# Decay exponents as sixteen products of 128 rows, with the weighing on VectorE

## The chip, the cores and the metric

The kernel runs on one core of a Trainium2 chip. The metric is the device time of one execution in microseconds. The names of the engines are those of the profile: PE is TensorE (its weight loads are PEld), DVE is VectorE, ACT is ScalarE, POOL is GpSimd, SP is SyncE, which issues most of the DMA transfers.

## The reference

One encoder layer over 256 positions and 2048 channels, in float32: a mixer, a gated convolutional MLP and an embedding block, each between RMS norms. Only the mixer matters here. One projection of the normalised input gives z (1024 channels), xbc (1536), dt (32) and u (1024). u goes through pooling windows and a small product per group. xbc goes through a convolution over five positions and a silu and is divided into xs (1024 channels, 16 heads of 64), B and C (two groups of 128 states each). Then comes a scan in chunks of 128 positions, once in each direction:

```python
da = dt * a                                   # a < 0
acum = jnp.cumsum(da, axis=-1)                # within a chunk of 128
cb = jnp.einsum("bclgn,bcsgn->bcgls", cmc, bmc)
seg = acum[..., :, None] - acum[..., None, :]
decay = jnp.exp(jnp.where(causal, seg, -jnp.inf))
y_diag = jnp.einsum("bcgls,bcgels,bcsgep->bclgep", cb, decay, xdt)   # xdt = xs * dt
decay_to_end = jnp.exp(acum[..., -1:] - acum)
states = jnp.einsum("bclgn,bcgel,bclgep->bcgepn", bmc, decay_to_end, xdt)
...
y = y_fwd + y_bwd + xs * d_skip               # then times silu(z), normed, projected
```

So every chunk, head and direction needs a 128x128 matrix of exponentials of differences of running sums.

## The kernel before, in words

**Arithmetic.** A float32 product is made of three faster products. `split` turns each weight block of 128x1024 into a high half, a cast on ACT (L150), and a low half, a subtraction on DVE (L151). PE then multiplies high by high, high by low and low by high. All of these go through the helper `mm`, so L87 is the line of nearly every product and they are told apart by the names of their outputs.

**Order.** The program's stages follow one another: the products for dt and u (`dtu`); three slabs of xbc, each of 512 channels and 192 products of 128x256, in the order 2 (B and C), 0, 1 (xs); z, in eight pairs of 24 products of 128x512; then the gate and norm of y, the output projection, the MLP and the embedding block. Each engine runs its own queue in an order that a scheduler fixed when the program was built. Small work is put among a stage's products by hand: `aside` takes one entry of the list `work` after each quarter of a slab, and after each pair of z, and runs its jobs.

**Buffers.** PSUM is divided into six tiles for the stages' sums (`main`) and two for everything else (`misc`): `seg`, `pool_mix`, `pool_map`, `cb`, `xs_turn`, `yo` and `yd` all use these two in turn. In SBUF there are 13 pages of 128x2048, five buffers each for high and low halves, and three raw ones.

**The mixer's small work.** After `dtu`, dt and `da` are made by small operations on DVE. `decays` makes the four vectors of decays to the chunk's ends (`dps`, `dec`). The exponents are made in eight parts of four heads each. `seg_prep(i)`, on POOL, multiplies masks with the high and low part of `da` (four operations of 128x512, L562), and `seg(i)` adds up both directions in one PSUM tile with four products; ACT takes the exponential into E (L571). For a pair of positions one of the two directions' exponents is zero there, since the masks select the other.

A slab's end is `xbc`: two products with the norm (`xr`, L409, DVE), a convolution of 16 instructions on DVE (L426), a tanh on ACT and one more DVE operation (L628). `cb` (L600) makes the products of C and B, masked by direction into `cbm`. `weigh(t, g)` makes `w`, the two directions' masked products times their dt: the first step on POOL (L634, 128x1024), then eight DVE operations of 128x128 (L639), then E times w (L643). `xs_turn` turns xs to have positions on partitions. `far(t)` weighs xs with the decay to the chunk's end (`xd`, POOL, L650), `skip(t)` starts y with xs times d (POOL, L654). `mix(t, g)` adds the part from the other chunk (`yo`, one product) and from the own (`yd`, eight products) to y.

The lists of jobs say where this stands. In slab 2: `seg_prep` 0 to 3, `pool_mix`, `decays`, `seg` 0. In slab 0: `seg_prep` 4 to 7, `seg` 1 to 4, `pool_map`, `cb`, `weigh(0, 0)`. In slab 1: `seg` 5 to 7, `xs_turn` of slab 0, the other three `weigh`. In z: after the fourth pair `xs_turn` of slab 1, after the fifth `far` and `skip`, then `mix`.

Of the kernel before, what the change touches and what calls it, by code (L numbers as in the profile page):

```python
# [11 lines left out]
F32 = mybir.dt.float32  # L12
F32R = mybir.dt.float32r
AF = mybir.ActivationFunctionType
ALU = mybir.AluOpType

P = 128
# [4 lines left out]
H = 16  # L22
# [29 lines left out]
def build(nc, a, out):  # L52
# [5 lines left out]
    with tile.TileContext(nc) as tc, \  # L58
# [12 lines left out]
        def page(name, dtype=F32):  # L71
            return gp.tile([P, 2048], dtype, tag="pg", bufs=13, name=name)
# [10 lines left out]
        def misc(name):  # L83
            return pc.tile([P, 512], F32, tag="misc", name=name)

        def mm(o, lhsT, rhs, start, stop):
            nc.tensor.matmul(o, lhsT, rhs, start=start, stop=stop, skip_group_check=True)  # L87


        ep = early.enter_context(tc.tile_pool(name="early", bufs=1))  # L90
# [18 lines left out]

        xt = [ep.tile([P, V_SCW + L], F32, name="xt0")] + [page(f"xt{i}") for i in (1, 2)]  # L110
        vt = cp.tile([P, V_N - V_SCW], F32, name="vt")
        small = ep.tile([P, 80 + 512], F32, name="small")

        last, sums_ = {}, {}

# [12 lines left out]

        last["dma"] = load(xt[0], a["x_cols"][:, :V_SCW + L])
        dtb, alog, dsk = small[:, :32], small[:, 32:64], small[:, 64:80]  # L130
        mask = small[:, 80:].rearrange("p (m f) -> p m f", m=4)

        def vec(i):
            return xt[0][:, i:i + 1] if i < V_SCW else vt[:, i - V_SCW:i - V_SCW + 1]
# [306 lines left out]
        for u in range(0, NK, 2):  # L441
            r = [wp.tile([P, 2048], F32, tag="raw", bufs=3, name=f"dtur{u}") if u else r0, page(f"dtur{u + 1}")]
# [37 lines left out]
        with tc.issue_after(half[0]), tc.issue_after(half[1]):  # L480
            xs_ = [page(f"x{t}") for t in range(2)]
            for t in range(2):
                load(xs_[t], x[t * P:(t + 1) * P, :])
            rx = row_rstd("rx", xs_)
            m_gt, m_lt = (ep.tile([P, P], F32R, name=n) for n in ("m_gt", "m_lt"))
            nc.vector.tensor_copy(m_gt, mask[:, 2, :])
            nc.vector.tensor_copy(m_lt, mask[:, 3, :])
            aneg = ep.tile([P, 32], F32, name="aneg")
            nc.scalar.activation(aneg, alog, AF.Exp)
            nc.gpsimd.tensor_scalar(aneg, aneg, -1.0, None, op0=ALU.mult)  # L490


            pt = page("pt")[:, :512].rearrange("p (k t) -> p k t", k=2)
            load(pt, a["p_t"])
            pth = cp.tile([P, 2, L], F32R, name="pth")
            ptl = cp.tile([P, 2, L], F32R, name="ptl")
            nc.scalar.copy(pth, pt)
            nc.vector.tensor_sub(ptl, pt, pth.bitcast(F32))
# [32 lines left out]
        nc.vector.tensor_scalar(e3, e3, 2.0, None, op0=ALU.mult)  # L531
        nc.vector.scalar_tensor_tensor(dtf, dtf, 0.0, e3, op0=ALU.max, op1=ALU.add)
        da = ep.tile([P, 2, 32], F32, name="da")
        dah = ep.tile([P, 2, 32], F32R, name="dah")
        dal = ep.tile([P, 2, 32], F32, name="dal")
        nc.vector.tensor_tensor(da, dt, aneg.unsqueeze(1).to_broadcast([P, 2, 32]), op=ALU.mult)
        nc.vector.tensor_copy(dah, da)
        nc.vector.tensor_sub(dal, da, dah.bitcast(F32))

# [8 lines left out]
                nc.gpsimd.tensor_mul(dec[:, d, :], dec[:, d, :], dt[:, d, d * H:(d + 1) * H])  # L550


        ee = [page(f"E{t}") for t in range(2)]
        steps = {}

        def seg_prep(i):
            t, q = divmod(i, 4)
            ap_ = page(f"ap{i}", F32R).rearrange("p (a h l) -> p a h l", a=4, h=4)
            for j in range(4):
                d, src = j // 2, (dah.bitcast(F32), dal)[j % 2]  # L560
                hs = slice(d * H + 4 * q, d * H + 4 * q + 4)
                nc.gpsimd.tensor_tensor(ap_[:, j], src[:, t, hs].unsqueeze(2).to_broadcast([P, 4, P]),  # L562
                                        mask[:, d, :].unsqueeze(1).to_broadcast([P, 4, P]), op=ALU.mult)
            steps[i] = ap_

        def seg(i):
            t, q = divmod(i, 4)
            sps, ap_ = misc(f"seg{i}"), steps.pop(i)
            for j in range(4):
                mm(sps, (m_gt, m_lt)[j // 2], ap_[:, j].rearrange("p h l -> p (h l)"), j == 0, j == 3)  # L570
            nc.scalar.activation(ee[t][:, q * 512:(q + 1) * 512], sps, AF.Exp)  # L571


        cat = Panel.__new__(Panel)
# [23 lines left out]
        xs = page("xs")  # L598
# [32 lines left out]
        def weigh(t, g):  # L631

            w = mid(f"w{t}{g}")
            nc.gpsimd.tensor_tensor(w.rearrange("p (h l) -> p h l", h=8),  # L634
                                    cbm[:, 1, g, t, :].unsqueeze(1).to_broadcast([P, 8, P]),
                                    dt[:, t, H + 8 * g:H + 8 * g + 8].unsqueeze(2).to_broadcast([P, 8, P]),
                                    op=ALU.mult)
            for h in range(8):
                nc.vector.scalar_tensor_tensor(w[:, h * P:(h + 1) * P], cbm[:, 0, g, t, :],  # L639
                                               dt[:, t, 8 * g + h:8 * g + h + 1], w[:, h * P:(h + 1) * P],  # L640
                                               op0=ALU.mult, op1=ALU.add)
            es = ee[t][:, g * 1024:(g + 1) * 1024]
            nc.vector.tensor_mul(es, es, w)  # L643

        def by_head(ap_, n=H):
            return ap_.rearrange("p (h c) -> p h c", h=n)

        def far(t):
            xd[t] = page(f"xd{t}")[:, :1024]
            nc.gpsimd.tensor_tensor(by_head(xd[t]), by_head(xs[:, t * 1024:(t + 1) * 1024]),  # L650
                                    dec[:, t, :].unsqueeze(2).to_broadcast([P, H, 64]), op=ALU.mult)

        def skip(t):
# [3 lines left out]
        def mix(t, g):  # L657
            c0 = t * 1024 + g * 512
            s = 1 - t
            po = misc(f"yo{t}{g}")  # L660
            mm(po, cbm[:, 2, g, s, :], xd[s][:, g * 512:(g + 1) * 512], True, True)
            tm = mid(f"ym{t}{g}")[:, :512]
            nc.vector.tensor_tensor(by_head(tm, 8), by_head(po, 8),
                                    dec[:, 2 + s, 8 * g:8 * g + 8].unsqueeze(2).to_broadcast([P, 8, 64]), op=ALU.mult)
            nc.gpsimd.tensor_add(y[:, c0:c0 + 512], y[:, c0:c0 + 512], tm)
            pd = misc(f"yd{t}{g}")
            for h in range(8):
                mm(pd[:, h * 64:(h + 1) * 64], ee[t][:, (8 * g + h) * P:(8 * g + h + 1) * P],
                   xs[:, c0 + h * 64:c0 + (h + 1) * 64], True, True)
            nc.vector.tensor_add(y[:, c0:c0 + 512], y[:, c0:c0 + 512], pd)  # L670

        def job(f, *args):
            return lambda: f(*args)

        xd = {}
        work.extend([
            [job(seg_prep, 0)],
            [job(seg_prep, 1), job(pool_mix, 0), job(pool_mix, 1)],
            [job(seg_prep, 2), job(pool_mix, 2), job(pool_mix, 3), job(decays)],
            [job(seg_prep, 3), job(seg, 0)],  # L680
        ])
        bc = xbc(2)
        work.extend([
            [job(seg_prep, 4), job(seg, 1), job(pool_map, 0), job(pool_map, 1)],
            [job(seg_prep, 5), job(seg, 2), job(cb, bc, 0), job(cb, bc, 1)],
            [job(seg_prep, 6), job(seg, 3), job(pool_map, 2), job(pool_map, 3)],
            [job(seg_prep, 7), job(seg, 4), job(weigh, 0, 0)],
        ])
        xa = xbc(0)
        work.extend([  # L690
            [job(seg, 5), job(weigh, 0, 1)],
            [job(seg, 6), job(xs_turn, xa, 0)],
            [job(seg, 7), job(weigh, 1, 0)],
            [job(weigh, 1, 1)],
        ])
        xb = xbc(1)
        y = page("y")
# [1 line left out]

        work.extend([  # L700
            [],
            [],
            [],
            [job(xs_turn, xb, 1)],
            [job(far, 1), job(skip, 0), job(far, 0), job(skip, 1)],
            [job(mix, 0, 0)],
# [291 lines left out]
def laid_out(a):  # L998

    def cols(*vs):  # L1000
        return np.concatenate([v.reshape(-1, P).T for v in vs], axis=1)

    return {
        "x_cols": np.concatenate([cols(a["mix_norm_pre"][0]),
                                  a["x"][0].T.reshape(NK, P, L).transpose(1, 0, 2).reshape(P, NK * L)], axis=1),
        "p_t": a["p"][0, 0].T.reshape(2, P, L).transpose(1, 0, 2),
        "columns": np.concatenate([
            cols(a["ssd_conv_w"][0], a["ssd_conv_b"][0], a["ssd_norm"][0], a["pool_scale"][0], a["ffn_norm_pre"][0],
                 a["ffn_conv_w"][0], a["ple_norm_pre"][0], a["ffn_conv_b"][0]),
            np.broadcast_to(np.concatenate([a[n][0].reshape(-1) for n in ("ssd_dt_bias", "ssd_a_log", "ssd_d")]),  # L1010
                            (P, 80)),
            masks().transpose(1, 0, 2).reshape(P, 4 * P)], axis=1),
    }


def masks():
    j = np.arange(P)[:, None]
    l = np.arange(P)[None, :]
    return np.stack([j <= l, j >= l, j > l, j < l]).astype(np.float32)


def constants():
# [17 lines left out]
```

## Time and profile before

| | |
|---|---|
| median of three runs | 1142.09 us (1141.17 to 1142.82) |
| profiled execution, its own time | 1140.26 us |
| its span | 1138.5 us |
| mean granted clock of TensorE | 0.995 |
| PE busy | 1115.9 us, 98% of the span |
| DVE busy | 935.8 us, 82% |
| ACT busy | 637.6 us, 56% |
| POOL busy | 128.9 us, 11% |

The span is the time from the first to the last recorded instruction of the profiled execution; 1.76 us lie around it, and the median of the runs is 1.83 us above this execution. The busy shares are means over stages with different limits. The stages that the change touches lie between 40 and 200 us: `dtu` ends at about 52 us, the slabs of xbc run to 151.59, and z to about 190. The chain that ended last is the work followed back from the last instruction, at each step to what released it.

### The profile page before, as it was taken

How to read it: one execution, taken by the hardware profiler on the slowest of the kernel's cores; microseconds unless marked ns; L12 is line 12 of the kernel's file. 1: busy time of each engine (PE TensorE's matmuls, PEld its weight loads, DVE VectorE, ACT ScalarE, POOL GpSimd, SP SyncE). 2: the span in 40 equal slices, each digit the busy share in tenths (PEclk: the TensorE clock that was granted, in tenths of full speed). 3: DMA queues.
4: the chain of work that ended last, by engine and by line, in shares of the span. 5: the costliest groups of instructions: out<-in, count | busy, mean ns of one | idle time of the engine just before them, and what ended most of it. 6: DMA issues, size and time to landing. Idle time of an engine off the chain costs nothing.

```text
span 1138.5 us, 15770 instructions
## 1 busy us (share of the span) xinstructions
PE 1115.9 (98%) x5982; PEld 962.5 (85%) x5982; DVE 935.8 (82%) x1277; ACT 637.6 (56%) x869; POOL 128.9 (11%) x124
## 2 busy tenths in 40 slices
PE   9998999999999999999999999999999999998996
PEld 9997987888888888888888888888888888886775
DVE  6579896699888877877877778867799999998795
ACT  7533543555674554544545545545677777776672
POOL 0274504200110100000000000000000000102001
PEclk9999999999999999999999999999999999999999
DMA  9952347545699999998999898966985589985673
GB/s 359 341 184 75 112 151 263 200 164 187 240 311 332 328 325 313 320 294 299 333 335 313 291 323 309 323 218 223 352 286 184 176 301 344 343 277 193 203 236 107
DMA packets 145419, 297.97 MB, mean 262 GB/s; under 512 B 5440, under 2 KB 98496, under 8 KB 137536
## 3 DMA queue, kind: packets, MB, share of 16 engines
q1 hardware_dynamic: 144784, 295.56, 76.4%
q0 software_dynamic: 272, 1.05, 0.5%
q8 instruction: 47, 0.77, 0.3%
q10 hardware_dynamic: 288, 0.36, 0.1%
q14 instruction: 28, 0.23, 0.1%
HBM read 266.54 MB, written 30.41 MB: 261 GB/s over the span
## 4 chain that ended last, share of the span: by engine, by line
PE 91%; DVE 5%; ACT 1%; DMA 1%; POOL 1%; issue 1%; DVEq 0%; POOLq 0%; ACTq 0%
PE va L87 22%; PE ga L87 21%; PE dna L87 15%; PE woa L87 7%; PE gt L87 4%; PE dtu L87 4%; PE z L87 4%; PE xbc L87 3%; PE dns L87 3%; DVE cv L426 2%; PE dn0s L87 1%; PE dn1s L87 1%; PE ple L87 1%; DMA gt04t<-gts 1%; DVE w L639 1%
## 5 line engine op out<-in xcount | busy, mean ns | idle before, releaser
L87 PE MATMUL ga<-wox,ug_0h 128*128 128x512 f32 x352 | 125.6, 395 | 0.0
L87 PE MATMUL ga<-wox,ug_1h 128*128 128x512 f32 x352 | 125.1, 394 | 0.0
L87 PE MATMUL va<-wox,uv_1h 128*128 128x512 f32 x352 | 124.8, 394 | 0.0
L87 PE MATMUL va<-wox,uv_0h 128*128 128x512 f32 x352 | 124.8, 394 | 0.0
L87 PE MATMUL ga<-wox,ug_1l 128*128 128x256 f32 x352 | 99.3, 282 | 0.0
L87 PE MATMUL ga<-wox,ug_0l 128*128 128x256 f32 x352 | 99.3, 282 | 0.0
L87 PE MATMUL va<-wox,uv_1l 128*128 128x256 f32 x352 | 99.2, 282 | 0.0
L87 PE MATMUL va<-wox,uv_0l 128*128 128x256 f32 x352 | 99.2, 282 | 0.0
L87 PEld LDWEIGHTS va<-wox,uv_1h 128*128 128x128 f32 x352 | 66.2, 188 | 14.8
L87 PEld LDWEIGHTS va<-wox,uv_0h 128*128 128x128 f32 x352 | 66.2, 188 | 14.8
L87 PEld LDWEIGHTS ga<-wox,ug_0h 128*128 128x128 f32 x352 | 66.2, 188 | 14.7
L87 PEld LDWEIGHTS ga<-wox,ug_1h 128*128 128x128 f32 x352 | 66.2, 188 | 14.7
L865 POOL TENSOR_TENSOR fc<-fc,rfb 128x1024 f32<-128x1024 f32 x11 | 28.0, 2546 | 438.6 <-ACT fc L864 438.6
L87 PEld LDWEIGHTS ga<-wox,ug_0l 128*128 128x128 f32 x352 | 66.3, 188 | 0.1
L87 PEld LDWEIGHTS ga<-wox,ug_1l 128*128 128x128 f32 x352 | 66.3, 188 | 0.0
L87 PEld LDWEIGHTS va<-wox,uv_0l 128*128 128x128 f32 x352 | 66.3, 188 | 0.0
L87 PEld LDWEIGHTS va<-wox,uv_1l 128*128 128x128 f32 x352 | 66.3, 188 | 0.0
L87 PE MATMUL dna<-dn_0h,hs 128*128 128x512 f32 x176 | 54.8, 394 | 0.0
L87 PE MATMUL dna<-dn_1h,hs 128*128 128x512 f32 x176 | 54.6, 393 | 0.0
L233 DVE TENSOR_TENSOR dnb<-dnb 128x1024 f32<-128x1024 f32 x22 | 28.0, 1271 | 16.1 <-DMA dnb<-w_ffn_down 16.1
L87 PEld LDWEIGHTS dna<-dn_1h,hs 128*128 128x128 f32 x176 | 33.1, 188 | 7.7
L87 PEld LDWEIGHTS dna<-dn_0h,hs 128*128 128x128 f32 x176 | 33.0, 188 | 7.6
(1866 smaller groups left out, 3136.0 us busy)
## 6 DMA issues: line engine op xcount, KB each, us to landing
dnb<-w_ffn_down SPq DMA_DIRECT2D x22, 1024.0 KB, 10.2
dns<-dnb SPq DMA_DIRECT2D x20, 1024.0 KB, 7.3
dn0r<-w_ffn_down SPq DMA_DIRECT2D x11, 1024.0 KB, 5.8
dn1r<-w_ffn_down SPq DMA_DIRECT2D x11, 1024.0 KB, 7.4
zr<-w_in SPq DMA_DIRECT2D x8, 1024.0 KB, 5.1
dtur<-w_in SPq DMA_DIRECT2D x14, 528.0 KB, 8.8
wo0r<-w_out SPq DMA_DIRECT2D x7, 1024.0 KB, 5.5
wo1r<-w_out SPq DMA_DIRECT2D x6, 1024.0 KB, 5.7
```

Source lines behind the costliest of these rows:

```text
L87: nc.tensor.matmul(o, lhsT, rhs, start=start, stop=stop, skip_group_check=True)
L233: nc.vector.tensor_add(v[:, 0:2], v[:, 0:2], v[:, 1::2])
L426: nc.vector.scalar_tensor_tensor(o[:, lo:hi], i[:, lo + d:hi + d], vec(wcol + j * wstep + f), o[:, lo:hi], op0=ALU.mult, op1=ALU.add)
L639: nc.vector.scalar_tensor_tensor(w[:, h * P:(h + 1) * P], cbm[:, 0, g, t, :], dt[:, t, 8 * g + h:8 * g + h + 1], w[:, h * P:(h + 1) * P], ...
L865: nc.gpsimd.tensor_tensor(cv.rearrange("p (f t) -> p f t", f=4), cv.rearrange("p (f t) -> p f t", f=4), rfb.unsqueeze(1).to_broadcast([P, ...
```

## The change

The exponents are written as differences of running sums. `seg_sums` makes these sums once: four products of 64 rows (`cps`) from `da4`, which holds da four times over and, for the second direction, negated. Two pages hold operands of 128 rows: `seg_x` with the sums' high and low parts and with ones, `seg_w` likewise with signs; their upper 64 rows are zero, so that products have the full 128 rows. Each is filled by ACT. Then each `seg(i)` is two products of 128x512, one for each direction, into two `misc` tiles; ACT copies the first to E, DVE takes the minimum of the two, and ACT the exponential. `seg_prep` goes, as do m_gt, m_lt, dah and dal. The first step of `weigh`, and `far`, go from POOL to DVE. `yo` is tied, in the order in which instructions are issued, behind the product that precedes it in the program. The jobs are dealt out anew.

```diff
 def mm(o, lhsT, rhs, start, stop):
-    nc.tensor.matmul(o, lhsT, rhs, start=start, stop=stop, skip_group_check=True)
+    last["pe"] = ins(nc.tensor.matmul(o, lhsT, rhs, start=start, stop=stop, skip_group_check=True))
...
-small = ep.tile([P, 80 + 512], F32, name="small")
+small = ep.tile([P, 89 + 512], F32, name="small")
...
+low, among, four = small[:64, 592:593], small[:64, 593:597], small[:64, 597:601]
...
-m_gt, m_lt = (ep.tile([P, P], F32R, name=n) for n in ("m_gt", "m_lt"))
-nc.vector.tensor_copy(m_gt, mask[:, 2, :])
-nc.vector.tensor_copy(m_lt, mask[:, 3, :])
+seg_w = page("seg_w", F32R)
+nc.scalar.activation(seg_w[64:], xs_[0][64:], AF.Copy, scale=0.0)
+seg_w = seg_w.rearrange("p (a q s) -> p a q s", a=4, q=4)
+seg_x = page("seg_x", F32R)
+nc.scalar.activation(seg_x[64:], xs_[0][64:], AF.Copy, scale=0.0)
+seg_x = seg_x.rearrange("p (a i l) -> p a i l", a=4, i=4)
+for a_ in range(4):
+    nc.scalar.activation(seg_w[:32, a_], four[:32].unsqueeze(2).to_broadcast([32, 4, P]), AF.Copy,
+                         scale=-1.0)
+    nc.scalar.copy(seg_x[32:64, a_], among[32:].unsqueeze(2).to_broadcast([32, 4, P]))
...
-nc.vector.tensor_copy(dah, da)
-nc.vector.tensor_sub(dal, da, dah.bitcast(F32))
+for d in range(2):
+    nc.vector.tensor_scalar(da4[:, :, d], da[:, :, d * H:(d + 1) * H].unsqueeze(2).to_broadcast([P, 2, 4, H]),
+                            1.0 - 2.0 * d, None, op0=ALU.mult)
...
-def seg_prep(i):
...
+def seg_sums():
+    cps = misc("cps")
+    for a_ in range(4):
+        mm(cps[:64, a_ * P:(a_ + 1) * P], da4[:, a_ // 2, a_ % 2].rearrange("p r h -> p (r h)"),
+           mask[:, 3 * (a_ % 2), :], True, True)
+    hi, c = page("seg_h", F32R)[:64, :512], page("seg_c")[:64, :512]
+    nc.scalar.copy(hi, cps[:64, :])
+    nc.vector.scalar_tensor_tensor(c, hi.bitcast(F32), low, cps[:64, :], op0=ALU.mult, op1=ALU.add)
+    c4 = c.rearrange("p (a l) -> p a l", a=4)
+    for i in range(4):
+        nc.scalar.activation(seg_x[:32, :, i, :], c4[:32], AF.Copy, scale=among[:32, i:i + 1])
+        nc.scalar.activation(seg_w[32:64, :, i, :], c4[32:], AF.Copy, scale=four[32:, i:i + 1])

 def seg(i):
     t, q = divmod(i, 4)
-    sps, ap_ = misc(f"seg{i}"), steps.pop(i)
-    for j in range(4):
-        mm(sps, (m_gt, m_lt)[j // 2], ap_[:, j].rearrange("p h l -> p (h l)"), j == 0, j == 3)
-    nc.scalar.activation(ee[t][:, q * 512:(q + 1) * 512], sps, AF.Exp)
+    ps = [misc(f"seg{i}{d}") for d in range(2)]
+    for d in range(2):
+        mm(ps[d], seg_w[:, 2 * t + d, q], seg_x[:, 2 * t + d].rearrange("p i l -> p (i l)"), True, True)
+    e = ee[t][:, q * 512:(q + 1) * 512]
+    nc.scalar.copy(e, ps[0])
+    nc.vector.tensor_tensor(e, ps[1], e, op=ALU.min)
+    nc.scalar.activation(e, e, AF.Exp)
...
 # weigh, first step
-            nc.gpsimd.tensor_tensor(w.rearrange("p (h l) -> p h l", h=8),
+            nc.vector.tensor_tensor(w.rearrange("p (h l) -> p h l", h=8),
 # far
-            nc.gpsimd.tensor_tensor(by_head(xd[t]), by_head(xs[:, t * 1024:(t + 1) * 1024]),
+            nc.vector.tensor_tensor(by_head(xd[t]), by_head(xs[:, t * 1024:(t + 1) * 1024]),
 # mix
-            mm(po, cbm[:, 2, g, s, :], xd[s][:, g * 512:(g + 1) * 512], True, True)
+            with tc.issue_after(last["pe"]):
+                mm(po, cbm[:, 2, g, s, :], xd[s][:, g * 512:(g + 1) * 512], True, True)
...
 work.extend([                                      # slab 2
-    [job(seg_prep, 0)],
-    [job(seg_prep, 1), job(pool_mix, 0), job(pool_mix, 1)],
-    [job(seg_prep, 2), job(pool_mix, 2), job(pool_mix, 3), job(decays)],
-    [job(seg_prep, 3), job(seg, 0)],
+    [],
+    [job(pool_mix, 0), job(pool_mix, 1)],
+    [job(pool_mix, 2), job(pool_mix, 3), job(decays), job(seg_sums)],
+    [job(seg, 0), job(seg, 1)],
 ])
 work.extend([                                      # slab 0
-    [job(seg_prep, 4), job(seg, 1), job(pool_map, 0), job(pool_map, 1)],
-    [job(seg_prep, 5), job(seg, 2), job(cb, bc, 0), job(cb, bc, 1)],
-    [job(seg_prep, 6), job(seg, 3), job(pool_map, 2), job(pool_map, 3)],
-    [job(seg_prep, 7), job(seg, 4), job(weigh, 0, 0)],
+    [job(seg, 2), job(pool_map, 0), job(pool_map, 1)],
+    [job(cb, bc, 0), job(cb, bc, 1), job(seg, 3)],
+    [job(seg, 4), job(pool_map, 2)],
+    [job(seg, 5), job(pool_map, 3)],
 ])
 work.extend([                                      # slab 1
-    [job(seg, 5), job(weigh, 0, 1)],
-    [job(seg, 6), job(xs_turn, xa, 0)],
-    [job(seg, 7), job(weigh, 1, 0)],
-    [job(weigh, 1, 1)],
+    [job(seg, 6), job(weigh, 0, 0)],
+    [job(seg, 7)],
+    [job(xs_turn, xa, 0), job(weigh, 0, 1)],
+    [],
 ])
 work.extend([                                      # z: first pairs
     [],
-    [],
-    [],
+    [job(weigh, 1, 0)],
+    [job(weigh, 1, 1)],
     [job(xs_turn, xb, 1)],
```

More of the change, by code (lines that the diff above doesn't have):

```diff
@@ L130, in build @@
         dtb, alog, dsk = small[:, :32], small[:, 32:64], small[:, 64:80]
-        mask = small[:, 80:].rearrange("p (m f) -> p m f", m=4)
+        mask = small[:, 80:592].rearrange("p (m f) -> p m f", m=4)
+        low, among, four = small[:64, 592:593], small[:64, 593:597], small[:64, 597:601]
         def vec(i):
@@ L533, in build @@
         da = ep.tile([P, 2, 32], F32, name="da")
-        dah = ep.tile([P, 2, 32], F32R, name="dah")
-        dal = ep.tile([P, 2, 32], F32, name="dal")
+        da4 = ep.tile([P, 2, 2, 4, H], F32, name="da4")
         nc.vector.tensor_tensor(da, dt, aneg.unsqueeze(1).to_broadcast([P, 2, 32]), op=ALU.mult)
-        nc.vector.tensor_copy(dah, da)
-        nc.vector.tensor_sub(dal, da, dah.bitcast(F32))
+        for d in range(2):
+            nc.vector.tensor_scalar(da4[:, :, d], da[:, :, d * H:(d + 1) * H].unsqueeze(2).to_broadcast([P, 2, 4, H]),
+                                    1.0 - 2.0 * d, None, op0=ALU.mult)
         dec = ep.tile([P, 4, H], F32, name="dec")
@@ L553, in build @@
         ee = [page(f"E{t}") for t in range(2)]
-        steps = {}
-        def seg_prep(i):
-            t, q = divmod(i, 4)
-            ap_ = page(f"ap{i}", F32R).rearrange("p (a h l) -> p a h l", a=4, h=4)
-            for j in range(4):
[L560 to L564, printed above, removed]
+        def seg_sums():
[10 more added lines that the diff above has]
+                nc.scalar.activation(seg_w[32:64, :, i, :], c4[32:], AF.Copy, scale=four[32:, i:i + 1])
         def seg(i):
             t, q = divmod(i, 4)
-            sps, ap_ = misc(f"seg{i}"), steps.pop(i)
-            for j in range(4):
-                mm(sps, (m_gt, m_lt)[j // 2], ap_[:, j].rearrange("p h l -> p (h l)"), j == 0, j == 3)
-            nc.scalar.activation(ee[t][:, q * 512:(q + 1) * 512], sps, AF.Exp)
+            ps = [misc(f"seg{i}{d}") for d in range(2)]
[5 more added lines that the diff above has]
+            nc.scalar.activation(e, e, AF.Exp)
         cat = Panel.__new__(Panel)
@@ L1011, in laid_out @@
                             (P, 80)),
-            masks().transpose(1, 0, 2).reshape(P, 4 * P)], axis=1),
+            masks().transpose(1, 0, 2).reshape(P, 4 * P), head_rows()], axis=1),
     }
@@ L1019, in masks, with head_rows @@
     return np.stack([j <= l, j >= l, j > l, j < l]).astype(np.float32)
+def head_rows():
+    p = np.arange(P)[:, None]
+    i = np.arange(4)[None, :]
+    return np.concatenate([-((p // 16) % 2), p % 4 == i, -1.0 * (p % 16 // 4 == i)], axis=1).astype(np.float32)
 def constants():
```

## The prediction

> **What bounds the kernel now.** I read the page's first part, then the chain that ended last, then PE's waits, then each engine's timeline around those waits.
>
> ```profile
> PE 1115.9 (98%) x5982; PEld 962.5 (85%) x5982; DVE 935.8 (82%) x1277; ACT 637.6 (56%) x869; POOL 128.9 (11%) x124
> PE 91%; DVE 5%; ACT 1%; DMA 1%; POOL 1%; issue 1%; DVEq 0%; POOLq 0%; ACTq 0%
> ```
>
> PE sets the time nearly everywhere, and from 330 to 800 us it is busy for 470.00 of 470. The change can win only by taking products off PE, or where the chain leaves PE. PE's waits (us in total, times, longest) and the chain (start, length, what) name the place:
>
> ```profile
> PE seg L87 <- DVE catl L189: 4.9, 1, 4.9
> PE dps L87 <- DVE mixt L585: 0.6, 1, 0.6
> PE xbc L87 <- DVE xb_0l L151: 0.5, 1, 0.5
> ```
>
> ```profile
> 84.01 13.44 DVE cv L426 x15
> ...
> 103.14 2.04 PE seg L87 x4
> 105.19 2.24 PE cb L87 x8
> 107.43 5.71 PE xbc L87 x48
> 113.14 0.94 PE seg L87 x4
> ...
> 151.59 22.26 PE z L87 x96
> ```
>
> PE stands 4.9 us before `seg`, because DVE is 13.44 us in one convolution. Then the same four products take 2.04 us that later take 0.94. Two rows of DVE's timeline say why the convolution is long:
>
> ```profile
> 83.94 14.23 DVE L426 SCALAR_TENSOR_TENSOR cv<-xr,vt,cv 128x254 f32<-128x254 f32 x16
> 125.51 6.39 DVE L426 SCALAR_TENSOR_TENSOR cv<-xr,vt,cv 128x254 f32<-128x254 f32 x16
> ```
>
> Sixteen equal instructions take 14.23 us, and 6.39 later. The table of windows has POOL busy 12.30 of 12.30 us at 83.90 to 96.20, and 0.00 of 6.30 at 125.50 to 131.80. POOL's groups show what it does in the first:
>
> ```profile
> L562 POOL TENSOR_TENSOR ap<-dal,small 128x512 fp32r<-128x512 f32 x16 | 22.4, 1400 | 0.0
> L562 POOL TENSOR_TENSOR ap<-dah,small 128x512 fp32r<-128x512 f32 x16 | 19.3, 1209 | 25.7 <-DVE dah L537 20.7 <-PE seg L87 5.0
> L634 POOL TENSOR_TENSOR w<-cbm,dt 128x1024 f32<-128x1024 f32 x4 | 8.5, 2120 | 23.5 <-DVE cbm L609 11.0 <-DVE cv L426 7.9 <-DVE E L643 3.0
> ```
>
> The change removes all 32 L562 operations and moves L634. From 152 to 186 us (z) PE never waits.
>
> **PE's products.** Removed: 32 `seg` products of 128x512, at 0.94/4 = 0.235 us: −7.5. Added: 16 of them, +3.8; four `cps` products of 64x128, between 0.11 (a 128x128 `xt` transpose, 0.87/8) and 0.23 (an `mx` product, 1.86/8), taken at 0.2: +0.8. PE is the bound, so all counts: −2.9.
>
> **PE's waits.** With L562 gone: `seg` behind `catl`, −4.9; the slow restart, 2.04 − 0.94 = −1.1; `cb`, whose first 0.8 us lay in the same stretch at clock 0.50, −0.4; and `dps` −0.6 and `xb_0l` −0.5, both waits for a DVE that is late. Sum with the products: 10.4. Each must hold with the new DVE work, so I walked DVE's new order.
>
> **DVE's work.** Added: 8 `min`, 0.69 us each by L670 (512 from PSUM), 5.5; 4 first steps of `w` and 2 `xd` of 128x1024, pitch 1.14 by L151, 6.8; `seg_c` and `da4` about 1.2. Four of those six read broadcasts of both operands; the other bound is POOL's own time (2.12 and 2.42). I take DVE's, since `ym`, with a broadcast, takes the 0.69 of plain ones. Removed: m_gt, m_lt, dah, dal, about 0.9, and the loss beside POOL, 7.8 in the first convolution alone. Until about 115 us that is enough: PE leaves slab 2 at 81.7 (before 81.4), passes `cb` at 100.2 instead of 107.43 and ends slab 0 at 114.3 instead of 123.25. From there DVE has hardly a pause, but its last xbc halves are ready at 134.4 and 137.6 where PE wants them at 135.5 and 138.4. z begins at 141.2 instead of 151.59: the 10.4.
>
> **z's entry.** Here slab 1's convolution, tanh product and weighing stand in DVE's queue between z's low halves. DVE starts at 141.2: xr 1.3, z2_0l 1.1, convolution 6.3, z2_1l 1.1, so 150.85; PE wants it after 40 products of 0.2325, at 150.5: wait 0.4. Then w, cv, eight L639 (2.17) and z4_0l: 156.35. PE is there after 52 products and eight transposes, at 154.55: wait 1.85. E and z4_1l end at 158.6, in time; so do the rest. In all 37.7 us of DVE work stand before 41.7 us of PE work.
>
> **What collides there.** `skip` stays on POOL and starts when the first `xs` copy after those transposes is written, near 154.9. The rows for that:
>
> ```profile
> 178.27 1.90 POOL L654 TENSOR_TENSOR y<-xs,small 128x1024 f32<-128x1024 f32 x1
> 180.13 2.88 POOL L650 TENSOR_TENSOR xd<-xs,dec 128x1024 f32<-128x1024 f32 x1
> 182.97 2.88 POOL L654 TENSOR_TENSOR y<-xs,small 128x1024 f32<-128x1024 f32 x1
> 181.41 2.68 DVE L151 TENSOR_TENSOR z_0l<-zr,z_0h 128x1024 fp32r<-128x1024 f32 x1 [0.16 <-ACT z_0h L150]
> ```
>
> Beside POOL a low half takes 2.68 us instead of 1.14; two skips cost DVE about 3.3. Then z4_0l comes at 157.9 (wait 3.35) and z4_1l at 161.75 (wait 1.3). All waits: 0.4 + 3.35 + 1.3, 5.1. Bounds: 2.25 without collision, 5.6 if DVE stands still through both (3.8).
>
> The Trainium skill ("SBUF — State Buffer", on who interferes with whom) calls the port that VectorE and GpSimd share an exclusive lock: an operation with two SBUF inputs and a GpSimd one shut each other out. By that the waits would be 5.6 and the gain 0.5 less. The trace has 2.68 instead of 1.14 beside POOL, not a full stop.
>
> **Edits priced at nothing.** ACT: two zero fills and eight small copies before slab 2's first split (2 x 1.81 + 8 x 0.48 = 7.5 us by rows of 2048 and 512) fill idle time of 6.52 and 1.34 us; `xb_0h` ends at 50.1 for a product due at 52.93, the tightest slack being 0.6. If the small ones cost double, 3.8 − 0.6 = 3.2 us would show. The eight seg_x/seg_w copies end at 83.15, needed at 84.2. Eight more `seg` copies lie in ACT's pauses (56% busy). `seg` now takes both `misc` buffers, so the next pair waits for a copy and a `min`; behind it on PE stand slab products, but other work lies between any two pairs. SP: xb2r's load goes ahead of pt, pmat, poolw; poolw, behind ACT's rxj at 38.2, is used only near 90. `small` has nine columns more. The tie of `yo`: it stands behind 144 z products in both kernels; from there all queues have the same order.
>
> **Sum.** 10.4 − 5.1 = 5.3: span 1138.5 − 5.3 = 1133.2. The profiled execution has 1.76 around its span: 1135.0. The median lay 1.83 above it: 1136.8.
>
> **Rivals.**
> *DVE keeps pace in z.* Collisions short, or skip falls between others: waits 0 to 2.25, gain 8.2 to 10.4, median 1131.7 to 1133.9. For it: in z, DVE's summed work is below PE's. Against: the queue's order, with convolution and weighing ahead of low halves.
>
> *The slow restart returns.* A wait of 3.35 us may be followed by half clock. The trace has such a wait late in the kernel:
>
> ```profile
> 1055.20:1056.20 1.00, 0.73 (x2) 0.64 (x3) 1.00 (x2) 1.00 (x2) 0.00 (x0) 0.50 0.99 418
> ...
> 1057.20:1058.20 1.00, 1.00 (x4) 0.71 (x4) 1.00 (x2) 0.94 (x2) 0.00 (x0) 0.50 0.02 8
> ```
>
> (Windows; the third number from the end is the granted clock.) After a PE wait of 3.36 us it is 0.50 for three microseconds. That would cost 3 x 0.5 = 1.5: median 1138.3. Against: low halves that are late give DVE the same time to catch up, so z4_1l's wait of 1.3 shrinks as PE slows. The Trainium skill ("TensorE: Matmul & The Clock Gate", the clock gate) gives the gate a free-running window of about 3.4 us and wants one of them idle, so whether such a wait is caught depends on where it falls; the trace's 3.36 was caught.
>
> *The long convolution is not POOL's doing.* Then DVE stays late, only the products (−2.9) come off, and DVE's additions take that back: about 1142. Against: 12.30 of 12.30 beside 14.23.
>
> *Slower: DVE as the bound.* Broadcast operands cost DVE what they cost POOL: w 4 x 0.98 + xd 2 x 1.28 = 6.5 us more, all between 115 us and `yo`, where slack is 1 us. Waits that long restart PE at half clock once, as above, +1.5. Gain 5.3 − 6.5 − 1.5 = −2.7: median 1144.8. From 5.3 us beyond the walk the kernel is slower than before, from 7.6 by more than 0.2%. For it: DVE has no pause from 115 on. Against: `ym`.
>
> **The numbers.** A measurement here tells apart 0.2%, 2.3 us: faster is below 1139.8, slower above 1144.4. Forecast 0.38, of which 0.03 falls into the middle band and 0.01 above; pace 0.18, all faster; restart 0.20, of which 0.14 is faster and 0.06 same; long convolution 0.05, same; DVE bound 0.19, of which 0.17 is slower and 0.02 same. Faster 0.34 + 0.18 + 0.14 = 0.66, same 0.03 + 0.06 + 0.05 + 0.02 = 0.16, slower 0.18. Range 1132 to 1146: the pace case's middle to just past the slow one.
>
> **What would show it.** After the change: the first L426 group near 6.4 us; no wait of `seg` or `cb` for DVE over 1 us; z's first product near 141, with PE waits for `z_1l` and `z_0l` of 0.4, 3 and 1 us near 150 to 162; POOL's two L654 beside DVE rows of 2.6 us; `yo` near 180.6 instead of 185.82; the same distances from there to the end. Wrong if `w` or `xd` takes 2 us on DVE alone, if xbc starts late behind ACT, or if `yo` comes at its old time.

## The result and the profile after

The changed kernel takes 1139.08 us (median of 20 runs, 1137.13 to 1140.63) and the kernel before 1141.53 us (20 runs); the ratio is 0.9975, with a 95% interval from 0.9968 to 0.9982. It is faster by 2.45 us, less than half of the 5.3 us that were forecast and just beyond the bound of 0.2% (2.3 us) that the prediction set. The profiled execution has a span of 1136.7 us instead of 1138.5.

The first part of the page and PE's waits of the changed kernel (us in total, times, longest):

```profile
span 1136.7 us, 15746 instructions
...
PE 1114.5 (98%) x5974; PEld 958.4 (84%) x5974; DVE 931.4 (82%) x1290; ACT 655.9 (58%) x896; POOL 77.0 (7%) x86
```

```profile
PE z L87 <- DVE z_1l L153: 3.2, 2, 2.7
PE z L87 <- DVE z_0l L153: 1.6, 1, 1.6
...
PE seg L87 <- ACT seg_x L579: 0.7, 1, 0.7
```

The wait of 4.9 us for `catl` is gone, and so are those behind `mixt` and `xb_0l`. In their place stand three waits in z, 4.75 us in all (0.45, 1.57 and 2.73), and a new one for ACT. POOL is busy for 77.0 us instead of 128.9. DVE's timeline of the first convolution (L428, L426 before):

```profile
87.16 1.76 DVE L428 SCALAR_TENSOR_TENSOR cv<-xr,vt,cv 128x254 f32<-128x254 f32 x4
88.84 0.68 DVE L589 TENSOR_TENSOR E<-seg,E 128x512 f32<-128x512 f32 x1
89.44 4.81 DVE L428 SCALAR_TENSOR_TENSOR cv<-xr,vt,cv 128x255 f32<-128x255 f32 x12
```

The 16 instructions take 1.76 + 4.81 = 6.57 us, where they took 14.23. Now z's entry, DVE's timeline again, and POOL's in the same stretch:

```profile
143.70 1.21 DVE L153 TENSOR_TENSOR z_0l<-zr,z_0h 128x1024 fp32r<-128x1024 f32 x1
144.83 6.39 DVE L428 SCALAR_TENSOR_TENSOR cv<-xr,vt,cv 128x254 f32<-128x254 f32 x16
151.15 1.22 DVE L153 TENSOR_TENSOR z_1l<-zr,z_1h 128x1024 fp32r<-128x1024 f32 x1
152.28 1.22 DVE L653 TENSOR_TENSOR w<-cbm,dt 128x1024 f32<-128x1024 f32 x1
...
154.55 2.18 DVE L658 SCALAR_TENSOR_TENSOR w<-cbm,dt,w 128x128 f32<-128x128 f32 x8
156.66 1.21 DVE L153 TENSOR_TENSOR z_0l<-zr,z_0h 128x1024 fp32r<-128x1024 f32 x1
...
162.34 5.47 DVE L658 SCALAR_TENSOR_TENSOR w<-cbm,dt,w 128x128 f32<-128x128 f32 x8
167.74 1.21 DVE L153 TENSOR_TENSOR z_1l<-zr,z_1h 128x1024 fp32r<-128x1024 f32 x1
```

```profile
156.63 9.46 POOL L673 TENSOR_TENSOR y<-xs,small 128x1024 f32<-128x1024 f32 x2 [79.84 <-ACT xs L637]
```

The convolution and the first weighing stand between low halves, as the walk had them. The second weighing takes 5.47 us instead of 2.18, beside `skip` on POOL; the low half behind it, z_1l, is the one that PE waits 2.73 us for. Then comes the clock. These are windows (PE's busy time first, the granted clock third from the end):

```profile
166.00:169.00 3.00, 0.27 (x2) 0.00 (x0) 3.00 (x9) 1.21 (x2) 0.09 (x1) 0.95 0.00 0
169.00:172.00 3.00, 3.00 (x7) 2.42 (x8) 3.00 (x3) 0.00 (x0) 0.00 (x0) 0.50 0.59 167
172.00:173.00 1.00, 1.00 (x5) 0.80 (x5) 1.00 (x2) 0.00 (x0) 0.00 (x0) 0.95 1.03 426
```

Three microseconds at 0.50 follow the wait; the window from 173 to 174 us is at 1.00 again. From the first `yo` on the two kernels are alike: in PE's timeline it starts at 183.69 (185.66 before), and 953.0 us follow it (952.8 before).

### The profile page after: what moved, and what is told of

Its sections match the earlier page's. It is cut to its first block, busy times and chain, and to the rows that moved or that the text cites. A ratio compares the mean times of both kernels' runs of the same rounds, so it can differ in the third digit from the quotient of the medians.

```text
span 1136.7 us, 15746 instructions
## 1 busy us (share of the span) xinstructions
PE 1114.5 (98%) x5974; PEld 958.4 (84%) x5974; DVE 931.4 (82%) x1290; ACT 655.9 (58%) x896; POOL 77.0 (7%) x86
## 4 chain that ended last, share of the span: by engine, by line
PE 89%; DVE 5%; DMA 2%; ACT 2%; issue 1%; POOL 1%; DVEq 0%; POOLq 0%; ACTq 0%
PE va L87 22%; PE ga L87 21%; PE dna L87 14%; PE woa L87 7%; PE gt L87 4%; PE dtu L87 4%; PE xbc L87 4%; PE dns L87 2%; PE z L87 2%; PE dn0s L87 1%; DMA dn1r<-w_ffn_down 1%; DVE w L658 1%; PE ple L87 1%; PE dn1s L87 1%; DMA gt04t<-gts 1%
```

## Experiments

The theory after the result: freeing POOL opens the stretch up to z as forecast; at z's entry most of that is lost to the order of DVE's queue, to the collision with `skip`, and to the half clock that follows. Rivals: DVE has too much work there in any order; the moved weighing, not `seg_prep`, brought the gain. Ratios are to the kernel before, with 95% intervals; "span" is that of the one profiled execution.

**POOL alone, in the kernel before.**

```diff
 def seg_prep(i):
     t, q = divmod(i, 4)
+    if i:
+        steps[i] = steps["kept"]
+        return
...
-    steps[i] = ap_
+    steps[i] = steps["kept"] = ap_
```

> The kernel before with `seg_prep` done once, for the first four heads, and its result used for all eight parts: 28 of POOL's 32 operations are gone, the products on PE stay (the output is not the reference's). Theory (POOL's work is what stretches DVE's first convolution, and that is PE's wait): its 16 instructions take 6.4 us instead of 14.2, the wait of 4.9 us and the half clock after it go, z begins at 144 to 145 instead of 151.59; the weighing stays on POOL in slab 1, so part of it may come back there or in z: span 1131 to 1135. Rival (the convolution is slow for another reason): it stays near 14 us, and the span at 1138.

Measured: 1133.62 us, ratio 0.9927 (0.9914 to 0.9939), span 1131.7. DVE's timeline, and all of PE's waits from 50 to 200 us:

```profile
82.63 6.39 DVE L426 SCALAR_TENSOR_TENSOR cv<-xr,vt,cv 128x254 f32<-128x254 f32 x16
```

```profile
PE xbc L87 <- DVE xb_0l L151: 0.4, 1, 0.4
PE yd L87 <- DVE y L673: 0.2, 1, 0.2
```

POOL's work is what stretched the convolution; without it the wait goes, z begins at 143.83 instead of 151.43, and z's entry has no wait: five low halves of z stand ahead of slab 1's convolution in this kernel's queue, three in the changed one. So one effect of the change, with all 32 `seg` products left on PE, is worth more than the whole change. By the start of xbc, z begins 91.25 us later here and 89.68 in the changed kernel (143.83 − 52.58 and 142.56 − 52.88): up to z the rest of the change, the halved products among it, is worth 1.57 us more. From z's first product to `yo` the order turns round: 34.23 us here, 41.13 there.

**The six operations moved to DVE, alone, in the kernel before.**

```diff
-nc.gpsimd.tensor_tensor(w.rearrange(...
+nc.vector.tensor_tensor(w.rearrange(...
...
-nc.gpsimd.tensor_tensor(by_head(xd[t]), ...
+nc.vector.tensor_tensor(by_head(xd[t]), ...
```

> The kernel before with only the first step of `weigh` and `far` moved to DVE, order of the jobs unchanged. Theory (seg_prep is what counts, these six operations are worth little): the first convolution stays at 14 us, the wait of 4.9 us stays, span 1137 to 1139. Rival (moving them was the gain): span below 1136.

Measured: 1143.09 us, ratio 1.0015 (1.0005 to 1.0024), span 1140.4. PE's waits:

```profile
PE seg L87 <- DVE catl L189: 4.9, 1, 4.9
PE z L87 <- DVE z_1l L151: 1.9, 1, 1.9
```

The convolution stays at 14.23 us and the wait at 4.9; a new wait of 1.9 us for a z_1l appears. The move alone brought no gain; it was a small loss, which the expected range had not held.

**They go back to POOL, in the changed kernel.**

```diff
-nc.vector.tensor_tensor(w.rearrange(...
+nc.gpsimd.tensor_tensor(w.rearrange(...
...
-nc.vector.tensor_tensor(by_head(xd[t]), ...
+nc.gpsimd.tensor_tensor(by_head(xd[t]), ...
```

> The changed kernel with the first step of `weigh` and `far` back on POOL. Theory (a POOL operation stops DVE about as long as DVE would take for the work itself, so that where it stands matters little): span within 2 us of the changed kernel's 1136.7, with L426-like or L658-like DVE rows stretched beside POOL. Rival 1 (moving them to DVE is what filled DVE at z's entry): 3 us or more faster. Rival 2 (moving them is what brought the gain): 2 us or more slower.

Measured: 1140.44 us, ratio 0.9989 (0.9981 to 0.9998), span 1137.6. PE's waits:

```profile
PE z L87 <- DVE z_1l L153: 5.2, 1, 5.2
```

Five low halves now stand ahead of the convolution, and PE gets through z to 163 us without a wait; but DVE waits 1.79 us for POOL's `w` and then has both weighings ahead of one low half. Three waits of 4.75 us became one of 5.24. The result lies within the 2 us of the theory; where these operations stand matters little, and they are not what fills z's entry.

**`skip` on DVE, in the changed kernel.**

```diff
-nc.gpsimd.tensor_tensor(by_head(y[:, t * 1024:(t + 1) * 1024]), ...
+nc.vector.tensor_tensor(by_head(y[:, t * 1024:(t + 1) * 1024]), ...
```

> The changed kernel with `skip` on DVE, behind `xd`, instead of on POOL. Theory (POOL's two skips stop DVE for 3.3 us in the eight weighing steps, that makes PE's wait of 2.7 us for z_1l, and that wait brings the half clock): the second group of L658 takes 2.2 us instead of 5.47, the wait of 2.7 us and the clock of 0.50 after it both go, `yo` comes 4.3 us earlier (2.7 + 1.6), less at most 0.4 us for the two skips on DVE: span 1132.4 to 1133. Rival (DVE simply has too much to do ahead of z's low halves, wherever skip is): the wait stays at 2 us or more or moves to another half, span 1136 to 1137.

Measured: 1135.89 us, ratio 0.9946 (0.9934 to 0.9959), span 1134.1. DVE's timeline and the windows:

```profile
162.67 2.20 DVE L658 SCALAR_TENSOR_TENSOR w<-cbm,dt,w 128x128 f32<-128x128 f32 x8
```

```profile
166.00:169.00 3.00, 3.00 (x14) 2.44 (x13) 3.00 (x3) 1.61 (x2) 0.00 (x0) 1.00 0.57 157
169.00:172.00 3.00, 3.00 (x14) 2.44 (x13) 3.00 (x4) 0.55 (x1) 0.00 (x0) 1.00 0.96 313
```

The weighing is short again, the wait of 2.73 us and the half clock are gone, the waits of 0.44 and 1.57 us stay. `yo` starts at 179.86, which is 3.83 us earlier, and 4.15 by the start of xbc (53.20 here, 52.88 there). The span missed its expectation by a microsecond: 954.2 us follow `yo` here, 953.0 in the changed kernel, though nothing was edited there. Among the twelve profiled executions that stretch lies between 952.8 and 955.1 us, so spans are compared no finer.

**The last two weighings later, in the changed kernel.**

```diff
 work.extend([                                      # z: first pairs
     [],
-    [job(weigh, 1, 0)],
-    [job(weigh, 1, 1)],
+    [],
     [job(xs_turn, xb, 1)],
-    [job(far, 1), job(skip, 0), job(far, 0), job(skip, 1)],
-    [job(mix, 0, 0)],
+    [job(far, 1), job(skip, 0), job(far, 0), job(skip, 1), job(weigh, 1, 0)],
+    [job(mix, 0, 0), job(weigh, 1, 1)],
...
```

> The changed kernel with the last two `weigh` after z's fourth and fifth pair and `xs_turn` after the third; skip stays on POOL. Theory (only the order of DVE's queue at z's entry is at fault): the waits of 1.6 and 2.7 us go, with them the half clock; 0.45 us behind the convolution stays: span 1136.7 - 1.6 - 2.7 - 1.6 = 1130.8, up to 1132.5 if the last weighing, now behind the first `yo`, holds up y's norm. Rival (volume of DVE work): other low halves come late, by 2 us or more in all, span above 1134.

Measured: 1133.19 us, ratio 0.9926 (0.9912 to 0.9939), span 1131.4. PE's waits in z:

```profile
PE z L87 <- DVE z_1l L153: 0.4, 1, 0.4
```

Only the wait behind the convolution is left. The collision now falls on two low halves at 170.61 and 173.39 (2.79 and 2.86 us), where DVE has slack. No work was removed, so the volume of DVE's work was not the cause. With the last weighing behind `yo`, PE waits 0.4 us before a `yd`, where the changed kernel waits 0.2.

**Both edits.**

> Both edits together: the late `weigh` and skip on DVE. Theory: the same gain as by the late weighing alone, within 0.5 us, since either takes the long wait away and the collision would now fall where DVE has slack: span 1130.5 to 1132. Rival (collisions cost wherever they fall): this one is faster than the late weighing alone by 2 us or more.

Measured: 1132.28 us, ratio 0.9923 (0.9909 to 0.9937), span 1130.1. The two intervals lie almost on each other, and from the start of xbc to `yo` both kernels take 124.56 us: once the order is right, moving skip adds nothing. The median is 9.4 us below that of the kernel before that ran beside it (1141.67), and 6.8 below the changed kernel. None of the other runs is faster by more than the intervals; the late weighing alone, and the two runs below that build on this one, cannot be told from it.

**All four weighings where the kernel before has them.**

```diff
 work.extend([                                      # slab 0
...
-    [job(seg, 5), job(pool_map, 3)],
+    [job(seg, 5), job(pool_map, 3), job(weigh, 0, 0)],
 ])
...
 work.extend([                                      # slab 1
-    [job(seg, 6), job(weigh, 0, 0)],
-    [job(seg, 7)],
-    [job(xs_turn, xa, 0), job(weigh, 0, 1)],
-    [],
+    [job(seg, 6), job(weigh, 0, 1)],
+    [job(seg, 7), job(xs_turn, xa, 0)],
+    [job(weigh, 1, 0)],
+    [job(weigh, 1, 1)],
 ])
```

(In z the entries of the second and third pair are empty.)

> The changed kernel with the four `weigh` where the kernel before has them (last quarter of slab 0, first, third and fourth of slab 1), skip on POOL. Theory (it is the order at z's entry, and slab 1 has room for two more weighings only in part): the waits of 1.6 and 2.7 us in z go, but slab 1's and z's first low halves come late by 1 to 3 us in all: span 1131.5 to 1134.5. Rival (DVE is full from 115 us on, so that work put earlier costs PE as much as it saves later): span 1136 or more.

Measured: 1143.67 us, ratio 1.0021 (1.0012 to 1.003), span 1142.7. The span lies in the rival's range, but neither picture held. Slab 1 is hardly late: z begins at 143.60, 0.46 later by the start of xbc. But PE's waits and DVE's timeline show:

```profile
PE z L87 <- DVE z_1l L153: 9.1, 1, 9.1
```

```profile
142.18 1.24 DVE L153 TENSOR_TENSOR z_0l<-zr,z_0h 128x1024 fp32r<-128x1024 f32 x1
...
148.87 6.50 DVE L428 SCALAR_TENSOR_TENSOR cv<-xr,vt,cv 128x254 f32<-128x254 f32 x16 [1.01 <-ACT cv L422]
155.28 1.22 DVE L153 TENSOR_TENSOR z_1l<-zr,z_1h 128x1024 fp32r<-128x1024 f32 x1
```

The weighing pushed z's first halves back in DVE's queue, until only one stands ahead of the convolution; the second comes behind it. Five ahead, as in the kernel before: no wait right behind the convolution. Three: 0.45 us in the changed kernel, 1.9 where the moved operations came alone. One: 9.1. So z's entry follows how many low halves DVE has made when the convolution begins, together with what stands right behind it; no run changed this number alone.

**The late start of z.** z's first product came later than forecast, and the wait of `seg` for ACT is part of it. Two ways to take it away: `seg` 0 and 1 a quarter of a slab later, tried in the changed kernel and in the one with both edits; and the four seg_w copies on DVE, tried in the one with both edits.

```diff
-    [job(seg, 0), job(seg, 1)],
+    [],
 ])                                                 # slab 2 ends
...
 work.extend([
-    [job(seg, 2), job(pool_map, 0), job(pool_map, 1)],
+    [job(seg, 0), job(seg, 1), job(seg, 2), job(pool_map, 0), job(pool_map, 1)],
```

> The changed kernel with `seg` 0 and 1 in the first quarter of slab 0 instead of the last of slab 2. Theory (the 0.7 us that PE waits for ACT's last seg_x copy is 0.7 of the 1.35 us by which z began later than forecast): the wait is gone and z begins at 141.8 instead of 142.5; at z's entry PE then waits as much longer, since DVE sets the time there, unless DVE's queue, too, is 0.7 us earlier: span 1135.5 to 1137. Rival: the two pairs of products now wait on each other's copies and minima, 1 us or more slower.

> Late weighing, skip on DVE and the late `seg` 0 and 1 together. Theory: with z's entry open, PE is the bound from 85 to 185 us and the 0.7 us show in full: span 1129.3 to 1130 against 1130.1 without the last edit. Rival (the late seg pairs cost what they save): 1130 to 1131.

Measured: 1139.86 us, ratio 0.9979 (0.997 to 0.9988), and 1133.81 us, ratio 0.9927 (0.9915 to 0.994). No gain: the wait for seg_x went, and in both a wait of 0.9 us came up for the copy of the pair before (`seg` for ACT's E, L588), so that z begins 0.5 us later by the start of xbc, not 0.7 earlier. Three pairs in one place wait on each other for the two `misc` buffers, as the rival had it. The spans, 1138.5 and 1131.2, are above what the theory gave; the medians show no loss beyond the intervals.

```diff
-nc.scalar.activation(seg_w[32:64, :, i, :], c4[32:], AF.Copy, scale=four[32:, i:i + 1])
+nc.vector.tensor_scalar(seg_w[32:64, :, i, :], c4[32:], four[32:, i:i + 1], None, op0=ALU.mult)
```

> The kernel with late weighing and skip on DVE (span 1130.1), and the four seg_w copies (0.72 us each on ACT) made by DVE, which stands idle from 82.7 to 86.5 there. Theory (ACT's eight copies are what `seg` 0 waits for): the 0.7 us wait goes, and the pairs behind it no longer wait for ACT: z begins 0.7 us earlier, at about 141.8, span 1129.2 to 1129.7. Rival (the rest of slab 0 takes it back, as with the late `seg` 0 and 1): 1130 or more.

Measured: 1132.81 us, ratio 0.9922 (0.9909 to 0.9936), span 1132.7. `seg` no longer waits, and z begins 89.21 us after the start of xbc instead of 89.69 (142.69 − 53.48 and 142.41 − 52.72). The gain of 0.5 us is too small for these runs: the times are the same. The span lies in the rival's range, but that is no evidence for it: of all executions, this one has the longest stretch behind `yo` (955.1 us).

## Why the prediction was right or wrong

The direction, the mechanism and the place of the loss were right; the size was not: 2.45 us instead of 5.3. Step by step:

- **POOL behind the long convolution:** right. 14.23 became 6.57 us, the wait of 4.9 us went, and the run with `seg_prep` once shows the cause alone.
- **Products on PE:** nearly right. The sixteen `seg` products came as priced; the four `cps`, which the trace records as eight products, took 1.02 us in the chain instead of 0.8.
- **z's start:** mis-sized. Forecast at 141.2, it came at 142.56. Of these 1.4 us, 0.7 is the wait for seg_x: its copies were priced at 0.48 us each, the pitch of rows with 512 elements, and 0.2 is cps. ACT's group shows what they cost, busy time and mean in ns:

```profile
L580 ACT ACTIVATE seg_w<-seg_c,small 32x512 fp32r<-32x512 f32 x4 | 2.9, 723 | 0.1
...
L495 ACT ACTIVATE seg_w<-small 32x512 fp32r<-32x512 f32 x4 | 2.5, 629 | 0.0
```

 Eight copies of 0.73 instead of 0.48 us, start to start, are 2.0 us, and the slack was 1.0. The eight constant fills were under-priced too (0.635), but ended in time for xbc, which began at 52.88. When `cb` ends in the chain (101.3 instead of 100.2), PE is 1.1 us late, 0.2 more than these two terms; the remaining quarter of a microsecond comes behind it. Neither was taken apart.
- **Waits in z:** right in sum, 4.75 instead of 5.1, with the parts displaced. The two skips did cost DVE 3.3 us, as priced, but not in z4's halves: they fell into the second weighing, so the waits were 0.45, 1.57 and 2.73 instead of 0.4, 3.35 and 1.3. That the sum agrees is in part luck, since skip began at 156.63 and not near 154.9, and the walk had it slow down other operations. The reading of 2.68 us as less than a full stop does not hold either: two operations of the weighing took 1.99 us each beside skip, instead of 0.3.
- **The clock:** here the forecast failed. The slow restart was priced at 1.5 us and put among the rivals, at 0.20, because it was left open whether a wait of 3.35 us would be caught, and whether DVE would catch up. It came, behind a wait of 2.73 us. Nine products from 169.00 to 172.59 took 3.59 us, against 9 x 0.2325 = 2.09: 1.5 us. The run with skip on DVE shows wait and slow clock go together.
- **The rest:** from 151.43 to 142.56 z's start gains 8.87; minus 4.75 and 1.5 that leaves 2.6, and `yo` shows 1.97. About 0.5 of the difference is how waits are counted: from the modelled end of the product before, which lies 0.16 us behind the start that the pitch would give the next, three times over.
- **Rivals:** DVE did not keep pace. Broadcast operands cost DVE nothing: `w` takes 1.22 us like a low half, two `xd` 2.35, where POOL took 2.12 and 2.42 each; so the slower case is out.
- **`yo`'s tie** was priced at nothing; no run without it was made, so that stays as argued.

The step to learn from is the forecast of z's entry as a sum of waits alone. The walk itself said that one of them would be over three microseconds, and the trace of before showed what follows such a wait. That price belonged into the sum.

## What to carry to other kernels

An engine with 11% busy time can set the pace of one with 82%: look for equal instructions that take different times, and at who else was busy then. When a wait upstream is removed, look at the queue of the engine that was late: which of its operations now stand ahead of those that the bound engine needs next; reordering two list entries was worth some 6 us here, more than the change itself. And a wait of PE is priced with the half clock behind it where the traces show one: here behind waits of 2.73 us and more, not behind those up to 1.88.

## What the runs showed of the hardware

- **DVE and POOL shut each other out, and not in turn.** POOL's first `skip` was 7.5 us long by the trace's row for L673 (1952 ns the shorter of the two, 7547 the longer), while DVE ran five operations of 1024 elements in a row, 1.21 us each, 156.66 to 162.34. Then two of DVE's eight 128x128 operations took 1.99 us each, about one whole skip, and the other six their usual 0.3. The Trainium skill ("SBUF — State Buffer", on who interferes with whom) says that one of the two blocks for the whole instruction of the other: these rows agree, with 1.99 beside 1.95. In the kernel before, low halves of 2.6 to 2.75 us alternated with POOL's operations instead; what decides who waits was not tried.
- **The clock fell behind a wait of 2.73 us,** to 0.50 for about three microseconds; behind 1.57 us in the same kernel, and 1.88 in the one with the moved operations alone, it stayed at 1.00. With `seg` 0 and 1 later, an equal wait of 2.74 us ended at 169.79 with the clock still at 1.00 in the window from 170 to 171; the windows from 171 to 174 have 0.53, 0.50 and 0.50. So the slow stretch need not begin with the end of the wait. The Trainium skill ("TensorE: Matmul & The Clock Gate", the clock gate) wants a whole idle window of about 3.4 us; here less was enough.
- **Small ACT operations on 32 partitions did not overlap.** 0.63 and 0.72 us long, they start 0.635 and 0.73 apart, where two `xs` copies of 128x512 (L637), 0.59 each, take 1.08 together. Whether the partitions, the broadcast or the scale does it was not tried.
